# Third and fourth token block's output projections as one group of seven block products

## The chip, the cores and the metric

The kernel runs on one core of a Trainium2 chip. The metric is the time of one execution in microseconds of device time; for the kernel before, three runs took 2120.65, 2122.04 and 2125.73 us, median 2122.04. A profiled execution gives times of single instructions in the same unit.

## The reference

One decoder layer over 2048 tokens of width 1024, float32. What is computed, cut to its core:

```
h   = x * (1 + scale) + shift                    # modulation from c
q, k, v, r, a = split(h @ w_in)                  # 4 heads, dk 128, dv 256
o   = gated linear attention(q, k, v, a)         # chunks of 64, state over chunks
o   = rmsnorm(o) * norm_g * silu(r)              # the gated value
y   = o @ w_o                                    # the output projection, 1024 x 1024
x1  = layer_norm(alpha * x + (1 + gate) * y)
u,g = split(modulated(x1) @ w_up)                # 2 x 2816
x2  = (silu(causal_conv3(u)) * g) @ w_down
out = layer_norm(alpha * x1 + (1 + gate2) * x2)
```

## The kernel before

Tokens stand in four blocks (`tb` 0 to 3) of 512. Every large product is done with three matmuls of a rounded and a rest part (`mm3`, L109 to L112: high x high, high x low, low x high); `split` (L103) makes the two parts of a tile, a cast on ScalarE (ACT, L104) and a subtraction on VectorE (DVE, L107). A *unit* is a piece of weights of 128x2x512 that stands in SBUF with both parts; it serves 24 matmuls of 128x512. `unit` (L156) hands out the next, and `issue` (L131) loads those ahead of it, two ahead of the one in use, into four buffers. A unit of the list `stream` can be loaded raw into half of its buffer and split there in place (`inplace`), can be stored after the split (`keep_in`), or can be loaded whole with both parts (`kept`).

Many products are made as two-by-two blocks with seven block products instead of eight: rows and columns of tokens, inner dimension and output columns are halved, sums of blocks are formed of both operands first, and the results are added into the outputs while they are accumulated in PSUM. The up and down projections and the q, k, v, r projections of other blocks are done so, and in the stage of this change the output projection of token blocks 0 and 1 (`o_pair`, L1481, operands from `o_x`, L1465, which takes the sums of gated values in SBUF). Its seven products stand in the order `OP` = 1, 0, 5, 6, 3, 4, 2 (L1194); the weights' sums come from `wfc_d`, the plain ones from `wf_d`, both folded with the gate.

The stage of this change stands between the input projections and the up projection and has 38 units: 8 for q and k of token block 1 (`q_segment`, L1443), 14 for `o_pair`, and 8 each for `o_segment` (L1509) of token blocks 2 and 3, which multiply plainly: eight k-tiles of gated values from DRAM (`g_d`, loaded by `get`, L1211) by `wf_d`, loaded again for each block and split again. Between the matmuls of the units stand the 16 heads of the attention (four blocks by four heads): each is a row of steps (`head_l` loads, `head_s` scales, `head_t` transposes, `head_a` masks, `head_b` states, `head_c` products, `head_n` norm, `head_d` transposes and gates; L1224 to L1384). The results of the projection are evicted by VectorE into rows of x (`load_z`, L1433), normalised (`ln1`, `normalise`, L1386 on), stored to `zn_d`, transposed on TensorE and stored to `xm2_d` (`ln1_kt`, L1410) as operand of the up projection. For block 3 the rows come back from `zn_d` during the up projection (`ln1_out`, L1425, table `todo`, L1752).

TensorE's order is written by hand: `at_unit` (L392) puts a step at a position counted in units, and `quarter` (L409) runs steps that are due after each quarter of a unit. `B0` is the stage's first unit; `H_AT`, `STEP`, `STEPB` (L1579 on) place the heads, `XO_AT` the operands of the first pair, `GET` those of the plain projections, `LZ_AT`, `LN_AT`, `LT_AT` rows, norm and transposes, `F_AT` (L1615) what prepares the up projection (`first_w`, `part_end` with `x_first(0)`, `x_first(1)`, `first_w1`, `first_w2`). For the other engines and the DMA issues, all of which are on SyncE's queue (SP), the framework's planner chooses an order with priorities: program order, drawn forward by `high_priority(offset)`. Issues on one queue run in order, and one that waits holds up those behind it. The up projection is a loop of 44 rounds (`n`); in its products, and in those of the q, k and r projections before the stage (`r_iter`), `keep` (L445) copies PSUM banks out by ACT (L448).

```
H_AT = (0.25, 1.5, 2.75, 4, 5, 6, 7.25, 8.25, 9.75, 13.5, 14.0, 15.5, 17.5, 19.5, 21.5, 23.5)
SEG = (("Q", 1), ("OO", 0), ("O", 2), ("O", 3))
```

## Time and profile before

| what | value |
|---|---|
| median of three runs | 2122.04 us |
| the profiled execution's own time | 2121.6 us |
| its span, first to last instruction | 2119.9 us |
| granted TensorE clock, mean | 0.996 |
| TensorE busy | 2085.8 us, 98% |
| VectorE busy | 1529.5 us, 72% |
| ACT busy | 1003.4 us, 47% |
| GpSimd busy | 107.0 us, 5% |
| DMA | 546.24 MB, mean 258 GB/s |

In the groups of the profile a line has source line, engine, operation, output and input tiles, shape and count, then busy time, mean ns of one, and idle time of the engine before them with what ended it. A line of waits has who waited for whom, microseconds in total, how often, and the longest. Matmuls overlap, so a matmul's own duration is longer than the step from one to the next. L12 is line 12 of the kernel before.

### The profile page before, as it was taken

To read this page: it belongs to the slowest core of one execution; us is meant where nothing else is said; L and a number is where in the kernel's file an instruction comes from. 1 tells how busy PE (TensorE), PEld (TensorE's weight loads), DVE (VectorE), ACT (ScalarE), POOL (GpSimd) and SP (SyncE) were. 2 spreads that over 40 slices of the span, in tenths; PEclk is the share of its full clock that TensorE was granted. 3 is DMA by queue.
4 is the path that set the end of the run, shared out by engine and by line. 5 is a ranking of instruction groups with operands and counts; after the bars stand their busy time and mean duration, and the time that the engine had idled before them with its cause. 6 is when DMAs were issued, how large, how long until landed. Compare 5 with 4: busy or idle time off the path is not lost.

```text
span 2119.9 us, 26188 instructions
## 1 busy us (share of the span) xinstructions
PE 2085.8 (98%) x9381; PEld 1721.9 (81%) x9381; DVE 1529.5 (72%) x2022; ACT 1003.4 (47%) x1405; POOL 107.0 (5%) x254
## 2 busy tenths in 40 slices
PE   9999999999999998999999999999999999999998
PEld 7887887778888787888888888888888888888886
DVE  6855757776687667878777787666676796577557
ACT  4648636674555544644444454333333443344332
POOL 0000000001112201100000000000000000020001
PEclk9999999999999999999999999999999999999999
DMA  9787888788745885777756679877777897677562
GB/s 336 304 295 261 283 306 286 268 306 317 277 145 196 310 289 192 274 249 285 273 194 219 219 253 321 288 258 273 246 276 256 295 325 250 206 247 251 189 200 89
DMA packets 192035, 546.24 MB, mean 258 GB/s; under 512 B 24928, under 2 KB 33504, under 8 KB 186272
## 3 DMA queue, kind: packets, MB, share of 16 engines
q1 hardware_dynamic: 191904, 544.56, 73.5%
q8 instruction: 74, 1.21, 0.2%
q14 instruction: 57, 0.47, 0.1%
HBM read 357.58 MB, written 186.91 MB: 257 GB/s over the span
## 4 chain that ended last, share of the span: by engine, by line
PE 71%; DVE 3%; ACT 2%; DMA 2%; issue 1%; POOL 1%; SPq 0%; DVEq 0%; POOLq 0%; ACTq 0%
PE ps_mm L110 15%; PE ps_mm L112 15%; PE ps_mm L111 15%; PE ps_w L111 7%; PE ps_w L110 7%; PE ps_w L112 7%; PE ps_w L1326 1%; PE ps_w L1354 1%; PE ps_w L1356 1%; PE ps_w L1310 1%; DMA hl<-wf_d 1%; DMA A<-a_d 0%; PE ps_w L1375 0%; PE ps_w L1416 0%; ACT on L1369 0%
## 5 line engine op out<-in xcount | busy, mean ns | idle before, releaser
L110 PE MATMUL ps_mm<-xc,hl 128*128 128x512 f32 x920 | 361.8, 393 | 6.2 <-ACT u L448 4.5
L111 PE MATMUL ps_mm<-xc,hl 128*128 128x512 f32 x920 | 359.5, 391 | 0.0
L112 PE MATMUL ps_mm<-xc,hl 128*128 128x512 f32 x920 | 358.8, 391 | 0.0
L110 PEld LDWEIGHTS ps_mm<-xc,hl 128*128 128x128 f32 x920 | 173.5, 189 | 46.4 <-ACT u L448 6.6
L112 PEld LDWEIGHTS ps_mm<-xc,hl 128*128 128x128 f32 x920 | 173.4, 189 | 36.5 <-DVE hl L107 0.2
L111 PEld LDWEIGHTS ps_mm<-xc,hl 128*128 128x128 f32 x920 | 173.6, 189 | 36.1 <-issue 0.5
L110 PE MATMUL ps_w<-xc,hl 128*128 128x512 f32 x464 | 180.6, 389 | 0.0
L111 PE MATMUL ps_w<-xc,hl 128*128 128x512 f32 x464 | 180.5, 389 | 0.0
L112 PE MATMUL ps_w<-xc,hl 128*128 128x512 f32 x464 | 180.5, 389 | 0.0
L1655 DVE SCALAR_TENSOR_TENSOR ct<-U,cw_sb,ct 128x512 f32<-128x512 f32 x176 | 131.8, 749 | 22.8 <-ACT ct L1649 20.2
L104 ACT CAST hl<-wu 128x1024 fp32r<-128x1024 f32 x90 | 94.8, 1053 | 104.1 <-PE ps_mm L112 76.9
L448 ACT COPY u<-ps_mm 128x512 f32<-128x512 f32 x112 | 65.3, 583 | 159.4 <-PE ps_mm L112 152.0
L104 ACT CAST dhl<-raw 128x1024 fp32r<-128x1024 f32 x57 | 60.1, 1054 | 159.2 <-PE ps_mm L112 98.5
L107 DVE TENSOR_TENSOR hl<-wu,hl 128x1024 fp32r<-128x1024 f32 x90 | 110.0, 1222 | 30.2 <-ACT hl L104 29.9
L107 DVE TENSOR_TENSOR dhl<-raw,dhl 128x1024 fp32r<-128x1024 f32 x57 | 69.7, 1223 | 65.4 <-ACT dhl L104 65.4
L107 DVE TENSOR_TENSOR hl<-raw,hl 128x1024 fp32r<-128x1024 f32 (+1 forms) x63 | 69.3, 1104 | 56.1 <-ACT hl L104 55.8
L110 PE MATMUL ps_mm<-hl,xg 128*128 128x512 f32 x240 | 104.0, 433 | 3.6 <-DVE z L1526 3.6
L104 ACT CAST hl<-raw 128x1024 fp32r<-128x1024 f32 (+1 forms) x63 | 60.0, 955 | 99.4 <-PE ps_mm L112 42.1
L104 ACT CAST hl<-wg 128x1024 fp32r<-128x1024 f32 x56 | 59.0, 1053 | 97.6 <-PE ps_mm L112 85.0
L110 PE MATMUL ps_mm<-dhl 128*128 128x512 f32 x264 | 102.7, 389 | 0.0
L111 PE MATMUL ps_mm<-dhl 128*128 128x512 f32 x264 | 102.7, 389 | 0.0
L112 PE MATMUL ps_mm<-dhl 128*128 128x512 f32 x264 | 102.7, 389 | 0.0
(284 smaller groups left out, 4743.7 us busy)
## 6 DMA issues: line engine op xcount, KB each, us to landing
hc_d<-ct SPq DMA_DIRECT2D x154, 256.0 KB, 2.9
raw<-hc_d SPq DMA_DIRECT2D x70, 512.0 KB, 4.2
draw<-wc_d SPq DMA_DIRECT2D x70, 512.0 KB, 4.6
wu<-in_wup_dram SPq DMA_DIRECT2D x44, 512.0 KB, 5.3
wg<-in_wup_dram SPq DMA_DIRECT2D x44, 512.0 KB, 4.3
wh_d<-hl SPq DMA_DIRECT2D x22, 1024.0 KB, 4.8
hl<-wh_d SPq DMA_DIRECT2D x22, 1024.0 KB, 6.6
mraw<-in_mws_dram SPq DMA_DIRECT2D x40, 512.0 KB, 6.0
```

What stands on the lines that cost most here:

```text
L104: accs["copy"] = nc.scalar.copy(h, src)
L107: return nc.vector.tensor_tensor(l, src if lsrc is None else lsrc, h.bitcast(F32), op=ALU.subtract)
L110: nc.tensor.matmul(po, a[0], b[0], start=first, stop=False, skip_group_check=resumed)
L111: nc.tensor.matmul(po, a[0], b[1], start=False, stop=False, skip_group_check=resumed)
L112: return nc.tensor.matmul(po, a[1], b[0], start=False, stop=last, skip_group_check=resumed)
L448: return t, nc.scalar.copy(t, po)
L1310: nc.tensor.matmul(pav[:, i], KI[:, s * P:s * P + P], Q[:, s], start=True, stop=True)
L1326: nc.tensor.matmul(pst[:, s % 2 * DV:s % 2 * DV + DV], KTt[:, s * P:s * P + P], v[s], start=True, stop=True)
L1354: nc.tensor.matmul(pos_, at[:, i], v[s], start=True, stop=st is None)
L1356: nc.tensor.matmul(pos_, Q[:, s, 0:128], st, start=False, stop=True)
L1655: nc.vector.scalar_tensor_tensor(ct, U[:, o + i:o + i + 512], cw_sb[:, j, i:i + 1], ct, op0=ALU.mult, op1=ALU.add)
```

## The change

The plain projections of token blocks 2 and 3 are replaced by a second call of `o_pair`, with 14 units; `o_segment` is gone. The operands `XY` are made as follows. Products 1 and 0 take the gated values of block 2 as they are (`y_x`). `y_sums` forms the sums of the gated values in SBUF, makes the operand of product 5 from one of them, and stores the other four (`xo_d`) to DRAM; `y_load` loads these into half of the operand's own tile when a tile is free, and `y_put` splits them in place. The gated values are no longer stored (`g_d` is gone), so they stay in SBUF until `y_sums`, in buffers shared with those of earlier blocks (`head_r`).

The weight parts of the first `o_pair`, once split, are stored to `wq_d` (1 MB each, 14 of them), and the second `o_pair` loads them with both parts and splits nothing.

The transposes of block 2 no longer stand in the stage: `todo` now runs `ln1_out` for block 2 in rounds 3 to 6 of the up projection and for block 3 in rounds 7 to 10 (before 3 to 6), and `x_pre` in rounds 12 and 15 (before 9 and 12).

Positions are set anew throughout: heads 6 and 8 to 15 stand up to two units earlier, the stage's tables are new, and steps before the stage (`x_prep`, gates, modulation, weight folding) move by up to some six units. Several priorities are raised (`keep` from 0 to 600, others from 60, 150, 300 or 600 to 300, 600 or 1200), the order in which buffers of units take turns no longer shifts at turn 48, and two of the raw tiles of `x_first` stand in the heads' buffers in place of those of the rows.

The diff, cut:

```diff
@@ -220,7 +220,7 @@
...
     e_d = [[dram.tile([P, 1024], F32, name=f"e_d{t}_{h}") for h in range(NH)] for t in range(NTB)]
-    g_d = [[dram.tile([P, 1024], F32, name=f"g_d{t}_{h}") for h in range(NH)] for t in range(NTB)]
+    xo_d = {i: [dram.tile([P, 1024], F32, name=f"xo_d{i}_{r}") for r in range(2)] for i in (2, 3, 4, 6)}
     xm2_d = [[dram.tile([P, 2, TB], F32, name=f"xm2_d{t}_{k}") for k in range(4)] for t in range(NTB)]
@@ -444,7 +444,7 @@
...
-        with tc.high_priority(offset=0):
+        with tc.high_priority(offset=600):
@@ -1137,19 +1137,19 @@
...
-        R_AT = ((7.75, 10.25, 12.0), (42.75, 45.0, 45.75))
+        R_AT = ((9.75, 10.25, 12.25), (42.75, 45.0, 45.25))
...
-        WAW_AT = (11, 46.25, 54.25)
+        WAW_AT = (12.25, 45.75, 53.75)
...
-        GR_AT = (17, 48, 54.75)
+        GR_AT = (17, 48, 54.25)
...
-        XP_AT = (18.5, 22.5)
+        XP_AT = (16.5, 19.75)
@@ -1157,28 +1157,28 @@
...
-        M_AT = (36, 37.5, 38, 39, 40, 41, 41.75, 43.25, 51, 52, 53, 54, 55, 56, 57, 58)
-        MF_AT = (50.5, 49.5, 56.5, 62.0)
+        M_AT = (36, 36.5, 37.75, 37.75, 40, 41, 41.75, 43.25, 51, 52, 53, 54, 55, 56, 57, 58)
+        MF_AT = (50.0, 49.5, 57.5, 62.5)
...
-        at_unit(65, mod2)
+        at_unit(68.5, mod2)
...
-        G_AT = (54, 55.5, 56.5, 56.75, 58, 59.25, 60, 61.5, 62.25)
+        G_AT = (51.75, 55.5, 56.5, 57.25, 58.5, 59.25, 60, 61.75, 62.5)
...
-        WF_AT = ((69, 69.5, 70, 70.75), (75, 75.5, 76, 76.5))
-        WM_AT = ((73, 74), (77, 78))
+        WF_AT = ((69, 69.0, 70.0, 70.75), (72, 74.25, 75.5, 76.75))
+        WM_AT = ((72.0, 74.0), (82.75, 83.75))
...
-        E_AT = (84, 85.45, 86.7, 87.7)
+        E_AT = (83.25, 85.45, 87.7, 88.45)
@@ -1193,12 +1193,14 @@
...
         wraw = {0: 0, 1: 2, 3: 6}
-        for i in OP:
-            for u in range(2):
-                stream.append((wf_d[wraw[i] + u] if i in wraw else wfc_d[i][u], None, None, True))
-        for tb in (2, 3):
-            for n in range(8):
-                stream.append((wf_d[n], None, None, True))
+        KEEP = (1, 1, 1, 1, 1, 1, 1, 1, 1, 1, 1, 1, 1, 1)
+        for q in range(2):
+            for n, (i, u) in enumerate((i, u) for i in OP for u in range(2)):
+                src = wf_d[wraw[i] + u] if i in wraw else wfc_d[i][u]
+                if q == 0:
+                    stream.append((src, wq_d[n] if KEEP[n] else None, None, True))
+                else:
+                    stream.append((None, None, wq_d[n], False) if KEEP[n] else (src, None, None, True))
         at_unit(B0 - 6, lambda: (load_unit(), load_unit()))
@@ -1210,12 +1212,11 @@
...
             kind, tb = key
-            assert kind == "Q" or ("g", tb, pr) in made
             t = xg_tile()
...
                 r = raw_tile("xraw")
-                load(r, xm1_d[tb][pr] if kind == "Q" else g_d[tb][pr])
+                load(r, xm1_d[tb][pr])
             split(t[:, 0], t[:, 1], r)
@@ -1284,12 +1285,11 @@
...
         def head_r(H):
-            if H["tb"] == 1:
+            tag = (("sra", "sra", "srb", "srb"), (None,) * 4, ("sr2", "sr2", "srb", "srb"), ("sra", "sra", None, None))[H["tb"]][H["h"]]
+            if tag is None:
                 sr = raw_tile("sr").rearrange("p (s c) -> p s c", s=2)
-            elif H["tb"] == 0:
-                sr = ab.tile([P, 2, 512], F32, tag="sr", name="sr", bufs=4)
             else:
-                sr = ab.tile([P, 2, 512], F32, tag="sr2", name="sr", bufs=2)
+                sr = ab.tile([P, 2, 512], F32, tag=tag, name="sr", bufs=2)
             H["sr"] = sr
@@ -1373,15 +1373,11 @@
...
                 nc.tensor.transpose(pt[:, s * P:s * P + P], on[:, s, e * P:e * P + P], ident)
-            with tc.high_priority(offset=300):
+            with tc.high_priority(offset=600):
                 nc.vector.scalar_tensor_tensor(sr[:, e], pt, ng_sb[:, e:e + 1], sr[:, e], op0=ALU.mult, op1=ALU.mult)
...
                 return
-            made.add(("g", H["tb"], H["h"]))
-            if H["tb"] < 2:
-                gated[H["tb"], H["h"]] = sr.rearrange("p s c -> p (s c)")
-            else:
-                store(g_d[H["tb"]][H["h"]].rearrange("p (s c) -> p s c", s=2), sr)
+            gated[H["tb"], H["h"]] = sr.rearrange("p s c -> p (s c)")
 
@@ -1478,9 +1474,41 @@
...
 
-        def o_pair():
+        XY = [None] * 7
+        yraw = {}
+
+        def y_x(i):
+            for pr in range(2):
+                x_put(XY, i, pr, gated[2, pr + 2 * i], xg_tile())
+
+        def y_sums(pr):
+            b11, b21, b12, b22 = [gated[b, pr + h] for b in (2, 3) for h in (0, 2)]
+            store(xo_d[2][pr], b22)
+            add(nc.vector, b11, b12, b11, SUB)
+            r = z_tile("xo")
+            add(nc.vector, r, b22, b11, SUB)
+            x_put(XY, 5, pr, r, xg_tile())
+            store(xo_d[4][pr], b11)
+            add(nc.vector, b12, b22, b12, SUB)
+            store(xo_d[6][pr], b12)
+            add(nc.vector, b21, b21, r, SUB)
+            store(xo_d[3][pr], b21)
+            made.add(("y", pr))
+
+        def y_load(i):
+            assert ("y", 0) in made and ("y", 1) in made
+            yraw[i] = [xg_tile() for _ in range(2)]
+            for pr, t in enumerate(yraw[i]):
+                load(t[:, 1].bitcast(F32), xo_d[i][pr])
+
+        def y_put(i):
+            for pr, t in enumerate(yraw[i]):
+                x_put(XY, i, pr, t[:, 1].bitcast(F32), t)
+
+        def o_pair(q):
             into = {1: (0, 0), 0: (0, 0), 5: (1, 0), 6: (1, 1), 3: (0, 1), 4: (1, 1), 2: (1, 0)}
             seen = set()
+            X = (XO, XY)[q]
             for i in OP:
@@ -1493,11 +1521,11 @@
...
                         for k in range(2):
-                            xh, xl = XO[i][2 * u + k]
+                            xh, xl = X[i][2 * u + k]
                             mm3(banks[t], (xh[:, tk], xl[:, tk]), (wv[:, 0, k], wv[:, 1, k]),
...
                         if u == 1:
-                            z = zs_of[tb][t][:, cs_]
+                            z = zs_of[2 * q + tb][t][:, cs_]
                             with tc.high_priority(offset=0):
@@ -1560,7 +1566,7 @@
...
-                    src[i] = actp.tile([P, D], F32, tag="zs", name="xs", bufs=5)
+                    src[i] = actp.tile([P, 2, 512], F32, tag=("E", "qk")[i - 4], name="xs").rearrange("p s c -> p (s c)")
@@ -1576,9 +1582,9 @@
...
-        H_AT = (0.25, 1.5, 2.75, 4, 5, 6, 7.25, 8.25, 9.75, 13.5, 14.0, 15.5, 17.5, 19.5, 21.5, 23.5)
-        STEP = (-0.4, 0, 0.5, 0.6, 0.75, 0.2, 0.5, 0.85, 1, 0.5, 1.5, 1.6, 1.6, 2.3, 2.5)
-        STEPB = (-0.5, 0, 0.5, 0.75, 1, 0.25, 0.75, 1, 1.25, 0.75, 1.75, 2, 2, 2.75, 3)
+        H_AT = (0.25, 1.5, 2.75, 4, 5, 6, 7, 8.25, 9.5, 12.75, 13.5, 14.75, 16.75, 18.5, 20, 21.5)
+        STEP = (-0.4, 0, 0.5, 0.6, 0.75, 0.2, 0.5, 0.85, 1, 1.5, 1.5, 1.6, 1.6, 2.3, 2.5)
+        STEPB = (-0.5, 0, 0.5, 0.75, 1, 0.0, 0.25, 0.75, 1.0, 0.5, 1.75, 2, 2, 2.75, 3)
@@ -1589,38 +1595,37 @@
...
-        SEG = (("Q", 1), ("OO", 0), ("O", 2), ("O", 3))
-        XO_AT = (7, 8.75, 11, 12.75, 14.75, 16.5, 18.5)
+        SEG = (("Q", 1), ("OO", 0), ("OO", 1))
+        XO_AT = (7, 8.75, 10.75, 12.75, 14.75, 15.5, 18.0)
...
-        GET = ((20.5, 20.5, 22.25, 22.25), (28.5, 29.5, 30.0, 31.0))
-        for n, key in enumerate(SEG[2:]):
-            for pr in range(4):
-                u = GET[n][pr]
-                if key[0] == "O":
-                    u = max(u, H_AT[4 * key[1] + pr] + STEPB[-1] + 0.05)
-                at_unit(B0 + u, get, key, pr)
-        LZ_AT = ((5.75, 5.75, 5.75, 5.75), (10, 10, 11, 11), (21.5, 21.5, 21.5, 21.5), (27.5, 27.5, 27.5, 27.5))
-        BY_ACT = ((0, 1, 0, 1, 0, 1, 0, 1), (0, 1, 0, 1, 0, 1, 0, 0), (0, 1, 0, 1, 0, 1, 0, 1))
-        LN_AT = ((17, 17.25, 17.5, 18.25), (21, 21.25, 21.5, 21.75), (29, 29.25, 29.5, 29.75))
-        LT_AT = ((18.5, 18.75, 19, 19.25, 19.5, 19.75, 20, 20.25), (22.0, 22.25, 22.5, 23.25, 23.5, 23.75, 24, 24.25), (30, 30.25, 30.5, 30.75, 31, 31.25, 31.5, 31.75))
+        YX_AT = (19.75, 21.75)
+        YS_AT = (23.0, 23.0)
+        for n in range(2):
+            at_unit(B0 + YX_AT[n], y_x, 1 - n)
+            at_unit(B0 + max(YS_AT[n], H_AT[14 + n] + STEPB[-1] + 0.05), y_sums, n)
+        YL_AT = ((25.5, 26.75), (27.25, 28.5), (29.0, 30.25), (31.0, 32.25))
+        for n, i in enumerate((6, 3, 4, 2)):
+            at_unit(B0 + YL_AT[n][0], y_load, i)
+            at_unit(B0 + YL_AT[n][1], y_put, i)
+        LZ_AT = ((5.75, 5.75, 5.75, 5.75), (10, 10, 10.75, 11), (21.5, 21.5, 21.5, 21.5), (25.75, 25.75, 25.75, 25.75))
+        BY_ACT = ((1, 1, 0, 0, 1, 0, 1, 1), (0, 1, 1, 0, 0, 0, 0, 0), (0, 0, 0, 1, 0, 1, 1, 1))
+        LN_AT = ((17, 18.25, 17.5, 18.0), (21, 21.25, 21.5, 21.75), (32.5, 32.75, 33, 33.25))
+        LT_AT = ((18.5, 18.75, 19, 19.0, 20.5, 20.75, 20, 20.25), (22.0, 22.25, 22.5, 23.25, 23.5, 23.75, 24, 24.25), (40.25, 40.25, 40.25, 38, 40, 40, 40, 40))
...
-            for kt in range(KT):
+            for kt in range(KT if tb < 2 else 0):
...
-        F_AT = (31, 32, 34, 35, 36)
+        F_AT = (28, 29.5, 34, 32, 34.5)
...
-                if kind == "OO":
-                    o_pair()
-                else:
-                    (q_segment if kind == "Q" else o_segment)(tb)
+                (o_pair if kind == "OO" else q_segment)(tb)
@@ -1749,8 +1754,8 @@
...
-        todo = {3 + pr: [(ln1_out, NTB - 1, None, (pr,), True)] for pr in range(4)}
-        todo |= {9: [(x_pre, 1, 0)], 12: [(x_pre, 1, 1)]}
+        todo = {3 + pr + 4 * b: [(ln1_out, 2 + b, None, (pr,), True)] for b in range(2) for pr in range(4)}
+        todo |= {12: [(x_pre, 1, 0)], 15: [(x_pre, 1, 1)]}
...
```

35 lines of the change are left out of this document (7 added, 28 removed).

## The prediction

> **What bounds the kernel now.** First I read the page: the busy row of the engines and the chain of waits. In the busy row the numbers are microseconds, share of the span and instructions.
>
> ```profile
> span 2119.9 us, 26188 instructions
> PE 2085.8 (98%) x9381; PEld 1721.9 (81%) x9381; DVE 1529.5 (72%) x2022; ACT 1003.4 (47%) x1405; POOL 107.0 (5%) x254
> PE 71%; DVE 3%; ACT 2%; DMA 2%; issue 1%; POOL 1%; SPq 0%; DVEq 0%; POOLq 0%; ACTq 0%
> ```
>
> TensorE is busy almost throughout, so a matmul that goes away is worth its issue step, as long as nothing else becomes late. The busy time of one matmul (389 ns) is not that step, because matmuls overlap. The timeline of TensorE has both: 36 block matmuls in a row, first and last row here, start 489.07 and 497.00 us.
>
> ```profile
> 489.07 0.39 PE L110 MATMUL ps_mm<-xg,hl 128*128 128x512 f32 x1
> ...
> 497.00 0.39 PE L112 MATMUL ps_mm<-xg,hl 128*128 128x512 f32 x1
> ```
>
> That is 7.93 us for 35 steps, so 0.2266 us a matmul and 5.44 us for a unit of 24 matmuls. I number the units of the stage from 0 (481.2 us: the first k-major unit of the second block's q and k): before there are 38, of which 22 to 37 are the projections of the third and fourth block.
>
> Next the windows of this stage (units 0 to 7, 8 to 21, 22 to 37; columns: length, then busy time of PE, PEld, DVE, ACT and POOL, granted clock, DMA share, GB/s), and what TensorE waited for, first in the time before 481 us, then in the stage.
>
> ```profile
> 481.20:573.70 92.50, 89.76 (x442) 76.47 (x441) 58.47 (x102) 44.74 (x97) 12.39 (x35) 1.00 0.83 298
> 573.70:722.84 149.14, 145.48 (x727) 122.89 (x726) 122.16 (x205) 78.38 (x160) 25.90 (x53) 1.00 0.60 209
> 722.84:849.60 126.76, 118.05 (x557) 96.50 (x556) 86.27 (x117) 60.34 (x89) 15.15 (x33) 0.99 0.71 254
> ```
>
> ```profile
> PE ps_mm L110 <- ACT u L448: 5.6, 6, 2.2
> PE ps_mm L110 <- ACT p L448: 1.6, 2, 1.1
> ...
> PE ps_w L1375 <- ACT on L1369: 4.7, 3, 1.8
> PE ps_mm L110 <- DVE z L1526: 3.6, 1, 3.6
> PE ps_w L1416 <- ACT zs L1397: 2.5, 3, 1.0
> PE ps_w L1299 <- DVE sr L1377: 2.0, 1, 2.0
> ```
>
> ```profile
> 850.00:1240.00 390.00, 390.00 (x1738) 323.26 (x1738) 308.65 (x417) 179.69 (x244) 13.34 (x52) 1.00 0.69 243
> 783.88:849.60 65.72, 60.35 (x273) 49.09 (x272) 47.80 (x55) 29.20 (x29) 5.31 (x12) 0.97 0.61 223
> ```
>
> Behind the stage, in the up projection (first row), TensorE waits for nothing; the last ten units of the stage are the second row. So all that can still be gained lies in matmuls, in 7.2 us of waits for ACT's copies (`keep`) and some 13 us of waits in the stage.
>
> One thing comes on top of a wait: the matmuls after it step by 0.43 us for a while.
>
> ```profile
> 169.17 0.50 PE L110 MATMUL ps_mm<-xc,hl 128*128 128x512 f32 x1 [2.18 <-ACT u L448]
> ...
> 170.26 0.63 PE L110 MATMUL ps_mm<-xc,hl 128*128 128x512 f32 x1
> 170.69 0.63 PE L111 MATMUL ps_mm<-xc,hl 128*128 128x512 f32 x1
> 169.00:172.00 3.00, 2.83 (x8) 2.23 (x9) 3.00 (x4) 2.76 (x6) 0.00 (x0) 0.60 0.64 231
> 831.90:834.90 3.00, 3.00 (x9) 2.33 (x8) 3.00 (x4) 0.00 (x0) 0.00 (x0) 0.50 0.00 0
> ```
>
> The granted clock is 0.60 and 0.50 there. Some seven matmuls lose 0.2 us each, 1.4 us a time; it follows two of the `keep` waits and the 3.6 us wait. The Trainium skill (TensorE: Matmul & The Clock Gate, What's actually happening) has the clock fall after an idle window of about 3.4 us; here a wait of 2.18 us was enough, so the row decides, and by the page alone the two `keep` waits would have been 2.8 us cheaper.
>
> **The change part by part.** (1) *Matmuls.* The two eight-unit projections become one group of seven products of two units: 16 units become 14. 48 matmuls x 0.2266 = **-10.9 us**. The first pair's projection already has this form in units 8 to 21.
>
> (2) *Transposes moved.* The third block's 32 transposes go from the stage into the up projection, where the fourth block's are already. The chain of waits gives a group's step there:
>
> ```profile
> 920.70 0.87 PE ps_w L1416 x8
> zc<-zn_d SPq DMA_DIRECT2D x16, 128.0 KB, 3.7
> 526.94 1.30 PE ps_w L1310 x8
> 529.62 1.73 PE ps_w L1326 x8
> 532.74 0.87 PE ps_w L1375 x8
> ```
>
> 32 x 0.87/8 = 3.5 us leaves and returns: 0. With them move 16 loads and 8 stores on SP (the fourth block's 16 loads land in 3.7 us each) and 8 evictions, now all on ACT, which is busy under half of that time; nothing waits for them before the second half of the up projection. What does go is the wait of such transposes for ACT's normalised rows at 800 us: two of the three waits of L1416 above, the longest of 1.0 among them, so 1.0 + 0.8 of 2.5 us: **-2 us**. If that cover is missing in the up projection, each lateness counts in full, since TensorE has no slack there; I keep 0 to +3.
>
> (3) *VectorE and ACT.* A 128x512 eviction costs 0.68 us, a split 1.05 us on ACT and 1.22 us on VectorE, a sum of two gated tiles 1.22 us:
>
> ```profile
> L107 DVE TENSOR_TENSOR hl<-hl 128x1024 fp32r<-128x1024 f32 x14 | 17.1, 1219 | 9.7 <-ACT hl L104 9.6
> L1389 DVE BATCH_NORM_STATS2 bst<-zs 128x6 f32<-128x512 f32 x13 | 8.3, 669 | 0.0
> L1526 DVE SCALAR_TENSOR_TENSOR zs<-zs,ps_mm 128x512 f32<-128x512 f32 x8 | 5.4, 682 | 0.0
> L352 DVE TENSOR_TENSOR xs<-xs 128x1024 f32<-128x1024 f32 x4 | 4.9, 1222 | 0.0
> L352 DVE TENSOR_TENSOR wu<-wu 128x512 f32<-128x512 f32 x1 | 0.7, 693 | 0.0
> ```
>
> Evictions 28 for 16 (+8.2 us), eight sums (+9.8), operand splits 14 for 8 (+7.3), weight splits 14 for 30 (-19.5), four block evictions less (-3): +3 us for VectorE over the stage, and ACT loses ten casts. What counts is where it falls. After the last head (position 24.5 of 36) there are 11.5 units, 62.6 us. VectorE then has 24 evictions (16.3), half to all of the sums and their splits (6 to 12), eight operand splits (9.8), statistics of the third block (8 x 0.67 + 0.8 = 6.2), the 16 sums and splits that build the up projection's operands (19.6), and its first weights (2.4 + 4 x 0.7 = 5.2): 63 to 69 us. It is full. Consecutive ones overlap by some 7%, so 59 to 65; with imperfect filling I take 5 us of TensorE wait, 0 to 15. It stands in the place of the 3.6 us wait for `z` and its 1.4 us of slow clock, which arise now at just this spot and for this reason: **0**.
>
> (4) *DMA.* In units 8 to 21 every weight part, once split, is stored (14 x 1 MB), and in units 22 to 35 it is loaded whole, 1 MB in place of 0.5 MB. The stores and loads of the gated values stay equal (16 of 0.5 MB). For 22 to 35 I add up: 12 weight loads (two are issued ahead) 12.6 MB, stores and loads of sums 4.2 + 4.2, rows of x 4.2, normalised rows 4.2, transposed rows 2.1, two gates 1.0, operands and weights of the up projection 6.3: 38.8 MB. TensorE needs for these units 14 x 5.44 = 76.2, plus what is left of heads 14 and 15 (a head is 1.30 + 0.87 by the rows under (2), 1.73 each for its states, its masked scores and its states' products, and 0.44 for four transposes, 7.8 in all; left are one head and 2.6) and 32 transposes (3.5) and switches between types (some 2): 92 us. So 38.8/92 = 420 GB/s is asked for. The nearest rows are the fullest 10 us and the busiest 50 us:
>
> ```profile
> 530.00:540.00 10.00, 10.00 (x53) 8.58 (x52) 6.36 (x12) 4.71 (x12) 0.58 (x4) 1.00 1.00 396
> 700.00:750.00 50.00, 46.92 (x241) 38.94 (x240) 36.15 (x63) 25.19 (x46) 9.29 (x22) 1.00 0.87 301
> 835.00:900.00 65.00, 65.00 (x288) 53.80 (x287) 57.99 (x79) 37.29 (x46) 6.51 (x17) 1.00 0.62 222
> ```
>
> The third block's normalised rows and one weight store (3.1 MB) may slip into the up projection, which has room (222 GB/s). 35.7 MB is 90 us at 396 GB/s and 119 us at 301: a lateness of 0 to 27 us. I take **+3 us**, near the upper rate, because the weights have a prefetch of two units (10.9 us against a landing of 6.6 us for 1 MB) and the queue mostly waited for buffers, not for transfers:
>
> ```profile
> SPq L141 <- PE ps_mm L112: 77.2, 19, 10.3
> hl<-wh_d SPq DMA_DIRECT2D x22, 1024.0 KB, 6.6
> wh_d<-hl SPq DMA_DIRECT2D x22, 1024.0 KB, 4.8
> ```
>
> The Trainium skill (DMA: Bandwidth & Descriptors, Where 436 GB/s comes from) has HBM bind at about 358 GB/s a core. The row of 396 GB/s is above that; by the page 35.7 MB would be 100 us, and the term +8 instead of +3.
> The 14 new stores stand in SP's one queue and wait for VectorE's half of the split; behind them stand the next weight load and the heads' loads. Units 8 to 21 have 209 GB/s and a DMA share of 0.60, so 14.7 MB more fits, and I take 0 there (-0 to +5).
>
> (5) *The way over DRAM.* Four of the seven operands go out and come back. From the last head's gate (24.5) to the product that needs the first of them (28) there are 19 us. The way takes 0.75 (gate) + 3 x 1.22 (sums) + 2.3 (split of the fifth operand) + 3.8 (store) + 5.5 (load) + 2.3 (split) = 18 us, durations from the rows here and below. Just hidden: **+1**, 0 to 5.
>
> ```profile
> g_d<-sr SPq DMA_DIRECT2D x8, 512.0 KB, 3.8
> xraw<-g_d SPq DMA_DIRECT2D x8, 512.0 KB, 5.5
> L1377 DVE SCALAR_TENSOR_TENSOR sr<-ps_w,ng_sb,sr 128x512 f32<-128x512 f32 x7 | 5.1, 747 | 4.2 <-PE ps_w L1375 4.2
> ```
>
> (6) *Priorities and positions.* `keep` is drawn forward on ACT (offset 0 to 600) and the steps before 481 us are set at other units. Bounds: all 7.2 us and 2.8 us of slow clock go (-10), or as much again is made elsewhere by the moved steps (+5). I take **-4**, the larger waits gone and some new small ones. The heads stand closer (16 by 24.5 instead of 26.5); their waits for ACT (4.7 us) I leave, -5 to +5.
>
> Sum: -10.9 - 2 + 0 + 3 + 1 - 4 = **-12.9 us**. The profiled execution took 2121.6 us (span 2119.9), 0.4 us under the median shown (2122.0). 2121.6 - 12.9 = 2108.7; I say 2109.
>
> **The rivals.** *More goes than the matmuls* (the copy waits and the head waits vanish, DMA costs nothing): -10.9 - 2 - 10 - 3 = -26 to -20, some 2098. For it: the first pair shows units without any wait on operands. Against: the last 11 units are full on VectorE.
> *VectorE becomes the bound of the last units.* Each split also waits 0.7 us on average for ACT's half (9.7 us over 14 in the row above). 14 such idle times on a full engine are 10 us more than I took: 2109 + 10 = 2119, no change that can be measured. For it: the 3.6 us wait arose there with less work (47.80 us busy in the last 65.72).
> *DMA becomes the bound of units 22 to 35* (the other side). If the queue moves no more than the 301 GB/s of the busiest 50 us, 35.7 MB takes 119 us against 92, +27 where I took +3: 2109 + 24 = 2133, slower. It decides from a landing of the 1 MB weight loads above 10.9 us, twice a unit; the loss passes the gain at about 320 GB/s. Against: the 301 GB/s came with a share of 0.87, not 1.00.
> *The change doesn't do what it says*: fewer matmuls are certain from the loops, so only their place could be wrong; I give that nothing of its own.
>
> **How the numbers follow.** A measurement of this kernel tells about 0.3%, 6.4 us, from no change: the borders are 2115.7 and 2128.4. My forecast (2102 to 2115) has 0.56, more gone 0.17, VectorE's bound 0.18, DMA's 0.09. Faster is the first two, 0.73; same 0.18; slower 0.09. The range runs from 2096 (most of "more gone") to 2123 (VectorE's bound with its upper spread) and leaves out some 0.15. The forecast's own range is 2102 to 2115.
>
> **What would show it.** Right: 9333 matmul records (48 fewer), 14 units from 22 to 35 in about 95 us, DMA in them at 350 to 400 GB/s, waits for L448 under 4 us before the stage, none in the up projection. Wrong: waits of block matmuls for weight loads (DMA, the new parts) of over a microsecond a unit, or for VectorE's operands at the products 6 and 3; weight loads that land after more than 10.9 us; or an up projection that begins with waits for its own operands.

## The result, and the profile after

The changed kernel took 2109.39 us (median of five runs, 2108.16 to 2115.09) against 2122.04 us (five runs, 2120.65 to 2126.9) for the kernel before on the same chip: ratio 0.9939, interval 0.992 to 0.9958, 12.65 us less. Predicted were 2109.0 us and faster. The total is right, by 0.4 us; several of its terms are not, and their errors nearly cancel, so that closeness is luck.

The busy row and the chain of waits of the page after:

```profile
span 2107.0 us, 26146 instructions
PE 2074.5 (98%) x9333; PEld 1713.0 (81%) x9333; DVE 1532.0 (73%) x2028; ACT 997.2 (47%) x1401; POOL 109.8 (5%) x254
PE 82%; DVE 6%; DMA 5%; ACT 4%; issue 2%; POOL 0%; SPq 0%; DVEq 0%; ACTq 0%; POOLq 0%
```

48 matmuls are gone, as counted in advance. TensorE is still busy for 98% of the span, and VectorE as long as it was (1529.5 us before, 1532.0 now, the 3 us more that the prediction counted). So what is left to find lies in places where TensorE waits.

The stage after in windows (units 0 to 7, 8 to 21, 22 to 35, then the last 11.5 units alone and 40 us inside them; columns as in the prediction):

```profile
484.49:573.73 89.24, 89.24 (x441) 76.56 (x440) 57.00 (x101) 43.61 (x97) 12.01 (x35) 1.00 0.92 332
573.73:729.92 156.19, 153.26 (x761) 129.79 (x759) 131.13 (x223) 83.90 (x175) 31.01 (x63) 0.99 0.81 296
729.92:826.99 97.07, 93.88 (x444) 77.49 (x443) 70.81 (x97) 37.37 (x57) 12.39 (x22) 1.00 0.90 335
764.30:826.99 62.69, 59.50 (x261) 48.20 (x260) 47.56 (x62) 20.84 (x20) 5.75 (x12) 1.00 0.86 332
760.00:800.00 40.00, 36.81 (x167) 29.48 (x166) 27.81 (x34) 9.07 (x11) 0.76 (x1) 1.00 0.99 377
```

Units 22 to 35 take 97 us (about 95 predicted) at 335 GB/s (350 to 400 predicted): 32.5 MB, where 35.7 were counted. Units 8 to 21 became 7 us longer than before, since more of the heads stand in them now, and carry the weight stores (209 GB/s before, 296 now) without harm. The waits of TensorE after: before the stage (first two rows), in the stage, and in the first 63 us of the up projection (last two rows):

```profile
PE ps_mm L110 <- ACT u L448: 9.4, 7, 3.2
PE ps_mm L110 <- ACT p L448: 0.5, 2, 0.3
...
PE ps_w L1375 <- ACT on L1369: 2.3, 3, 1.0
PE ps_mm L112 <- DVE xg L107: 1.5, 1, 1.5
PE ps_mm L110 <- DVE z L1533: 0.9, 1, 0.9
PE ps_mm L110 <- DVE zs L352: 0.8, 1, 0.8
PE ps_w L1299 <- DVE sr L1377: 0.3, 1, 0.3
...
PE ps_w L112 <- DVE hl L107: 2.0, 1, 2.0
PE ps_mm L110 <- ACT xc L104: 0.7, 1, 0.7
```

Three things are to be seen. The copy waits (L448) before the stage didn't shrink. TensorE's idle time in the stage (length less busy time, summed over the three windows) fell from 15.1 to 6.1 us. And the up projection, which began without any wait before, now waits for its own operands.

To compare kernels stretch by stretch I use one measure. The *nominal* time of a stretch is its matmuls, each by the usual step of its shape (0.2266 us for 128x512); the *excess* is the rest of the time from start to start: waits, slow clock after them, and switches between types. It comes from one profile of each kernel.

| kernel | median us | ratio to before, interval | excess before stage | units 0–7 | units 8–21 | from 22 on | first 60 us of up projection |
|---|---|---|---|---|---|---|---|
| before | 2122.04 | | 17.9 | 3.9 | 7.4 | 14.0 | 0.0 |
| after | 2109.39 | 0.9939, 0.992–0.9958 | 21.2 | 0.6 | 8.0 | 4.9 | 5.9 |
| e_plain | 2113.65 | 0.9964, 0.9948–0.998 | 21.6 | 0.9 | 6.6 | 3.7 | 0.0 |
| e_plainH | 2122.49 | 1.0005, 0.9994–1.0016 | 22.3 | 1.0 | 12.5 | 11.7 | 0.0 |
| e_plainP | 2115.91 | 0.9975, 0.996–0.999 | 16.4 | 0.6 | 11.3 | 3.5 | 0.0 |
| b_tr | 2121.77 | 0.9998, 0.9989–1.0007 | 16.1 | 3.0 | 8.7 | 13.3 | 0.0 |
| e_prekeep0 | 2110.88 | 0.9943, 0.9926–0.9961 | 22.7 | 1.4 | 6.8 | 4.9 | 7.2 |
| e_nokeep | 2113.86 | 0.9961, 0.9947–0.9976 | 18.9 | 0.9 | 9.4 | 9.6 | 5.9 |
| e_dma | 2120.64 | 0.9989, 0.9978–1.0 | 27.0 | 1.4 | 6.4 | 14.1 | 5.4 |
| e_xf | 2112.06 | 0.9948, 0.9935–0.9961 | 14.9 | 0.9 | 5.9 | 12.0 | 4.3 |
| e_ln | 2108.59 | 0.9936, 0.9919–0.9954 | 20.0 | 0.9 | 10.9 | 5.3 | 6.4 |
| e_nostat | 2110.12 | 0.9941, 0.9927–0.9954 | 23.5 | 0.6 | 6.0 | 6.8 | 6.4 |
| e_act | 2113.94 | 0.9961, 0.9947–0.9974 | 23.0 | 0.7 | 9.0 | 10.3 | 7.6 |
| e_actln | 2111.14 | 0.9951, 0.9936–0.9965 | 20.1 | 0.9 | 9.8 | 11.0 | 5.0 |

The kernel before ran again beside each group of experiments, with medians from 2121.4 to 2122.1 us; the ratios are to those. The column before the stage scatters from 14.9 to 27.0 us among the kernels that have the changed program there (all but before, b_tr and e_prekeep0). So a difference of a few microseconds in that column of single profiles tells nothing. A profiled execution need not lie at the median either: that of e_plainP took 2110.2 us, 5.7 us under it, that of e_xf 5.4 us under, those of e_act and e_plainH 4.7 and 3.3 us over theirs. Gains are therefore taken from the medians, and the columns only say where in the kernel the time lies.

### The profile page after: what moved, and what is told of

The parts are those of the page before. It is cut to its first block, busy times and chain, and to the rows that moved or that the text cites. A ratio compares the mean times of both kernels' runs of the same rounds, so it can differ in the third digit from the quotient of the medians.

```text
span 2107.0 us, 26146 instructions
## 1 busy us (share of the span) xinstructions
PE 2074.5 (98%) x9333; PEld 1713.0 (81%) x9333; DVE 1532.0 (73%) x2028; ACT 997.2 (47%) x1401; POOL 109.8 (5%) x254
## 4 chain that ended last, share of the span: by engine, by line
PE 82%; DVE 6%; DMA 5%; ACT 4%; issue 2%; POOL 0%; SPq 0%; DVEq 0%; ACTq 0%; POOLq 0%
PE ps_mm L110 17%; PE ps_mm L112 17%; PE ps_mm L111 17%; PE ps_w L112 8%; PE ps_w L111 8%; PE ps_w L110 8%; PE ps_w L1354 1%; PE ps_w L1326 1%; PE ps_w L1356 1%; PE ps_w L1310 1%; DMA A<-a_d 1%; DMA mraw<-in_mws_dram 1%; PE ps_w L1412 1%; DVE hl L107 1%; PE ps_w L1375 1%
## 5 line engine op out<-in xcount | busy, mean ns | idle before, releaser
L110 PEld LDWEIGHTS ps_mm<-xc,hl 128*128 128x128 f32 x920 | 173.5, 189 | 50.6 <-ACT u L448 10.9
L448 ACT COPY u<-ps_mm 128x512 f32<-128x512 f32 x112 | 65.3, 583 | 161.9 <-PE ps_mm L112 153.4
L112 PEld LDWEIGHTS ps_w<-xc,hl 128*128 128x128 f32 x464 | 87.1, 188 | 20.5 <-DVE hl L107 2.4
```

The costliest lines, as they stand in the source:

```text
L110: nc.tensor.matmul(po, a[0], b[0], start=first, stop=False, skip_group_check=resumed)
L112: return nc.tensor.matmul(po, a[1], b[0], start=False, stop=last, skip_group_check=resumed)
L448: return t, nc.scalar.copy(t, po)
```

## Experiments: which edit brings the time

**The seven products taken back (e_plain).** Everything of the change stays (positions, priorities, gated values in SBUF, transposes of the third block in the up projection), but the second pair is multiplied in sixteen plain units with operand positions of their own, no weights are kept, the buffers of units take turns as in the kernel before, and what prepares the up projection stands about two units later.

```diff
-        SEG = (("Q", 1), ("OO", 0), ("OO", 1))
+        SEG = (("Q", 1), ("OO", 0), ("O", 2), ("O", 3))
-        for q in range(2):
+        for q in range(1):
...
+        for tb in (2, 3):
+            for n in range(8):
+                stream.append((wf_d[n], None, None, True))
...
-        F_AT = (28, 29.5, 34, 32, 34.5)
+        F_AT = (31.25, 32, 34, 35, 36)
```

> The changed kernel with its second pair made plainly again: 16 units with eight products in place of 14 with seven, gated values still taken from SBUF, weights loaded and split (none kept), the positions of the heads and of all earlier steps as in the changed kernel; steps at the end of the stage two units later. Theory (a matmul that goes away is worth its step): 48 matmuls x 0.2266 = 10.9 us more than the changed kernel's 2109.4, less up to 4 us of waits that go with the fuller last units: 2116 to 2120. Rival (the positions made the gain, the seven products only moved the bound to VectorE and DMA): within 3 us of the changed kernel, 2107 to 2112.

Measured: 2113.65 us, 4.3 us above the changed kernel and 8.4 below the one before, between the two expectations. By the profile, e_plain has 10.9 us more nominal time in the stage than after, but 2.3 us less excess there and 5.9 us less at the start of the up projection. So the seven products save what was counted, and 8.2 us of it return as excess in the two profiles, 6.6 us by the medians (10.9 - 4.3). Of the 2.3 us some 1.5 are one stretch of slow clock (634.1 to 637.5 us in after), which another execution can lack; the 5.9 us are what stays. The other 8.4 us of the gain come without the seven products.

**The heads' positions taken back as well (e_plainH).** On top of e_plain, the positions of the heads, of the first pair's operands and of the norms and transposes of block 0 are those of before, and so is the choice of the engine that evicts the transposes of blocks 0 and 1 (`BY_ACT`).

```diff
-        H_AT = (0.25, 1.5, 2.75, 4, 5, 6, 7, 8.25, 9.5, 12.75, 13.5, 14.75, 16.75, 18.5, 20, 21.5)
+        H_AT = (0.25, 1.5, 2.75, 4, 5, 6, 7.25, 8.25, 9.75, 13.5, 14.0, 15.5, 17.5, 19.5, 21.5, 23.5)
...
-        XO_AT = (7, 8.75, 10.75, 12.75, 14.75, 15.5, 18.0)
+        XO_AT = (7, 8.75, 11, 12.75, 14.75, 16.5, 18.5)
```

> The second pair in sixteen plain units with the priorities of the changed kernel, but with the positions of the heads' steps, of the first pair's loads and of the first norms as in the kernel before. Theory (the new positions of the heads are what took the stage's excess from 25 to 11 us): the excess over the stage goes back to 19 to 25 us, and the time to 2117 to 2122 us. Rival (the priorities, or the other buffers of the gated halves, did it): the excess stays at 10 to 15 us, the time at 2112 to 2116 us.

Measured: 2122.49 us, as long as the kernel before. The stage's excess goes from 11.2 to 25.1 us, where before has 25.3. The waits in the stage, first of e_plain, then of e_plainH, show it:

```profile
PE ps_w L1375 <- ACT on L1369: 2.3, 3, 1.0
PE ps_mm L110 <- DVE z L1558: 1.8, 1, 1.8
```

```profile
PE ps_w L1375 <- ACT on L1369: 6.8, 4, 3.1
PE ps_mm L110 <- DVE z L1558: 1.8, 1, 1.8
...
```

The largest is the heads' wait for ACT's normalised output (`on`), which was 4.7 us before. The rest of the excess is slow clock behind such waits (three stretches in this profile's stage, one of them of double length, and none in that of e_plain) and steps without a listed wait; 5.9 us of the 13.9 come in units 8 to 21 and 8.0 from unit 22 on, where more heads stand when they are spread as before. The intervals of e_plain and e_plainH don't touch: what was set back (heads, first operands, first norms and transposes with their engine; they weren't separated) is worth about 9 us.

**The priorities taken back (e_plainP).** e_plain with the priorities of seven places in the stage as before (two of them here).

```diff
@@ head_l, head_t, head_a, state, head_c, head_d, copies in q_segment @@
-            with tc.high_priority(offset=1200):
+            with tc.high_priority(offset=60):
...
-            with tc.high_priority(offset=600):
+            with tc.high_priority(offset=150):
```

> The second pair in sixteen plain units with the new positions, but with the priorities of the seven places in the stage (head's first rows, transposes, mask, state, gate, the evictions of the weights' last part) as in the kernel before. Theory (positions alone did it): the excess over the stage stays at 10 to 15 us, and the time at 2112 to 2116 us. Rival (the priorities did it): the excess goes back to 19 to 25 us, and the time to 2117 to 2122 us.

Measured: 2115.91 us, 2.3 us over e_plain with intervals that overlap widely; the stage's excess is 15.4 us. The positions carry most of the gain; a share of the priorities of 2 or 3 us stays open.

**The transposes alone (b_tr).** The kernel before, with only the third block's transposes moved to the up projection.

```diff
-            for kt in range(KT):
+            for kt in range(KT if tb < 2 else 0):
...
-        todo = {3 + pr: [(ln1_out, NTB - 1, None, (pr,), True)] for pr in range(4)}
-        todo |= {9: [(x_pre, 1, 0)], 12: [(x_pre, 1, 1)]}
+        todo = {3 + pr + 4 * b: [(ln1_out, 2 + b, None, (pr,), True)] for b in range(2) for pr in range(4)}
+        todo |= {12: [(x_pre, 1, 0)], 15: [(x_pre, 1, 1)]}
```

> The kernel before with one part of the change alone: the third block's 32 transposes run in rounds 3 to 6 of the up projection, the fourth's in rounds 7 to 10, and the preparation of the second half in rounds 12 and 15. Theory (the transposes' own 3.5 us leave and return, and only the waits of these transposes go): 1 to 3 us faster than the kernel before, 2119 to 2121. Rival (they make room for VectorE and ACT ahead of the full end of the stage, so that the 5 us of wait and slow clock there go as well): 2114 to 2117.

Measured: 2121.77 us, no difference (the interval reaches from 2.3 us faster to 1.5 us slower). The waits in its stage:

```profile
PE ps_mm L110 <- DVE z L1526: 5.4, 1, 5.4
PE ps_w L1375 <- ACT on L1369: 4.6, 3, 1.8
```

The waits of L1416 for normalised rows are gone, as said, but the wait for `z` is 5.4 us in place of 3.6: VectorE's lateness at the end of the stage is met elsewhere.

**The time before the stage (e_prekeep0).** The changed kernel with the positions before the stage and the priority of `keep` as before.

```diff
-        with tc.high_priority(offset=600):
+        with tc.high_priority(offset=0):
...
-        R_AT = ((9.75, 10.25, 12.25), (42.75, 45.0, 45.25))
+        R_AT = ((7.75, 10.25, 12.0), (42.75, 45.0, 45.75))
```

> The changed kernel with all steps ahead of the stage at the positions of before and the bank copies (keep) at priority offset 0 again. Theory (these two parts of the change cost 3.3 us, since the stage begins at 484.5 us and not at 481.2): the stage begins at about 481.2 again, 2106. Rival (the copies' priority helps inside the up projection or at its start, or the positions help the stage): 2109 to 2113.

Measured: 2110.88 us, not to be told from 2109.39. The stage begins at 486.1 us, not at 481.2 as the theory had it. These edits neither bring nor cost anything that six runs show.

## Experiments: what the limits are worth

**No kept weights (e_nokeep).** Weights of the second pair are loaded raw and split again.

```diff
-        KEEP = (1, 1, 1, 1, 1, 1, 1, 1, 1, 1, 1, 1, 1, 1)
+        KEEP = (0,) * 14
```

> The changed kernel without keeping the weight parts: nothing is stored in units 8 to 21, and the second pair loads 0.5 MB raw for each unit and splits it. Theory (VectorE is the full engine of the last units): 14 more splits, 17 us of VectorE and 15 us of ACT in a stretch of 97 us with VectorE busy for 70.8: 3 to 10 us slower than the changed kernel, 2112 to 2119. Rival (DMA, with a share of 0.90 in these units, sets their pace): 22 MB less to move, 2 to 5 us faster, 2104 to 2107.

Measured: 2113.86 us, 4.5 us longer; the intervals still overlap at their ends, but the profile agrees. Units 22 to 35 in this kernel:

```profile
729.31:831.07 101.76, 94.50 (x444) 77.06 (x442) 86.65 (x111) 50.27 (x70) 13.45 (x22) 1.00 0.75 271
```

VectorE is busy for 86.65 of 101.76 us, against 70.81 of 97.07 with kept weights, and ACT for 50.27 against 37.37. The load on DMA falls from 335 to 271 GB/s, and no gain from that is to be seen. So keeping the weights in DRAM seems to pay because it relieves VectorE and ACT; which of the two counts, this run doesn't separate.

**More DMA (e_dma).** The changed kernel with 14 more transfers of 0.5 MB, DRAM to DRAM, one written into each of the units 22 to 35; nothing reads them, and so nothing ties them to those units.

```diff
+                    if q == 1:
+                        junk(u + 2 * OP.index(i))
...
+        def junk(n):
+            load(junk_d[n], wf_d[n % 8])
```

> The changed kernel with an additional transfer of 0.5 MB from DRAM to DRAM in each of the units 22 to 35, 7.3 MB in all, whose data nobody reads. Theory (DMA is used to 0.90 in these units, but the two units of prefetch hide that; the spare is about 0.10 x 97 us x 380 GB/s = 3.7 MB): the rest, 3.6 MB, is 10 us of queue, of which some arrives at TensorE as waits for weights and operands: 2112 to 2122. Rival (DMA is far from deciding): 2108 to 2111.

Measured: 2120.64 us, 11.3 us longer. But the transfers didn't go where they were meant to go. All 14, with first and last start, and those issued from 735 to 841 us:

```profile
L1542 SPq DMA_DIRECT2D junk_d<-wf_d x14: 473/538/975, 397.4 to 827.9; - x14
junk_d<-wf_d SPq DMA_DIRECT2D x4, 512.0 KB, 10.8
```

The planner issued ten of them before unit 22 (three at 397 to 413 us, seven at 606 to 685 us) and four at 812 to 828 us. The window of units 22 to 35, and from the timelines the largest new wait and the casts of the last product's operands:

```profile
734.91:841.10 106.19, 97.26 (x444) 78.99 (x443) 72.20 (x98) 36.52 (x56) 14.03 (x22) 0.97 0.95 357
825.54 0.47 PE L110 MATMUL ps_mm<-hl,xg 128*128 128x512 f32 x1 [3.56 <-ACT hl L104]
822.16 1.98 ACT L104 CAST xg<-xg 128x1024 fp32r<-128x1024 f32 x2
```

9.2 of the 11.3 us lie in these units (excess 14.1 instead of 4.9): units 33 and 34 take 9.2 and 10.2 us instead of 5.4. The casts of the last product's operands on ACT (third row) start at 822.16 us, in after at 809.57. The operands' loads land after 8.3 us (median, 785 to 830 us) instead of 5.0, and in this kernel the planner also has the scaling of the last rows and casts for the up projection ahead of these casts. The wait's row names the cast behind them, of a weight, which ends at 825.09 us; an eviction on VectorE ends at 825.44, so which of the two let the matmul go stays open. So neither theory nor rival was put to the test: the 11 us are the price of this order of the queues, with four more transfers in units 32 to 34, and how much room DMA has in units 22 to 35 isn't shown.

## Experiments: the start of the up projection

The first half of the up projection's operands (`x_first(0)`, called from `part_end`) is made at unit 29.5, the second (`x_first(1)`) at 32. Loads of the second half stand on SP's queue behind the stores of the normalised rows, and its eight operations on VectorE behind the last evictions. VectorE after, at the boundary (826.99 us), where each row is one or two operations and brackets hold idle time:

```profile
825.83 0.69 DVE L352 TENSOR_TENSOR z<-z,ps_mm 128x512 f32<-128x512 f32 x1 [0.67 <-PE ps_mm L112]
827.26 1.23 DVE L107 TENSOR_TENSOR hl<-wu,hl 128x1024 fp32r<-128x1024 f32 x1 [0.74 <-ACT hl L104]
828.40 1.22 DVE L352 TENSOR_TENSOR xs<-xs 128x1024 f32<-128x1024 f32 x1
829.54 0.68 DVE L352 TENSOR_TENSOR z<-z,ps_mm 128x512 f32<-128x512 f32 x1
830.14 1.22 DVE L352 TENSOR_TENSOR xs<-xs,xc 128x1024 f32<-128x1024 f32 x1
831.27 1.22 DVE L107 TENSOR_TENSOR hl<-wg,hl 128x1024 fp32r<-128x1024 f32 x1
```

The second half's work begins at 828.40 us, after the up projection itself. The longest wait there, the 2.0 us for `hl`, ends with the split in the last row: a weight part of the up projection, which stands behind two of the second half's sums. Five runs look for what holds it.

**Both halves earlier (e_xf).**

```diff
-        F_AT = (28, 29.5, 34, 32, 34.5)
+        F_AT = (26.75, 27.0, 34, 32, 34.5)
```

> The changed kernel with the first half of the up projection's operands made from position 27.0 (its first weights from 26.75) in place of 29.5 and 28. Theory (VectorE is idle for some 9 us between 784 and 803 us, while the loads of this half stand on the DMA queue behind loads that wait for operand buffers, and is then full from 803 to 850, which makes the waits at the start of the up projection): the loads leave some 15 us earlier, VectorE fills its idle time, the 5.9 us at the start of the up projection shrink to 2 or less: 2104 to 2107. Rival (DMA is full from 760 to 800 us, with a share of 0.99, and only passes the lateness on to weights or operands): 2108 to 2113, with waits of block matmuls inside the stage in their place.

Measured: 2112.06 us. The start of the up projection loses 4.3 us instead of 5.9, but in the stage there are new waits for the operands of the second pair:

```profile
PE ps_mm L112 <- DVE xg L107: 3.1, 1, 3.1
PE ps_mm L110 <- ACT xg L104: 2.5, 1, 2.5
```

The work of VectorE and ACT only changed places: units 29 and 30 take 8.3 and 11.0 us, in after 5.4 and 7.2.

**The norm of the last rows later (e_ln).** Its stores no longer stand ahead of the loads.

```diff
-        LN_AT = (..., (32.5, 32.75, 33, 33.25))
+        LN_AT = (..., (34.25, 34.5, 34.75, 35))
```

> The changed kernel with the third block's four norms at positions 34.25 to 35 in place of 32.5 to 33.25, behind the second half of the up projection's operand step at 34. Theory (the norms' stores wait for ACT on the one DMA queue, from 807 to 820 us, and hold up the four loads behind them, so that the up projection begins with 5.9 us of waits and slow steps): the loads leave earlier, 2 to 5 us faster, 2104 to 2107. Rival (VectorE is full from 803 us to 850 us whenever the loads come): no change, 2108 to 2111.

Measured: 2108.59 us, no difference that can be told. The loads leave at 815.7 and 816.1 us instead of 820.5 and 823.5, and VectorE begins the second half at 826.10 us, 3.3 us before the boundary (829.38 us) instead of 1.4 us behind it. TensorE's wait for VectorE's `hl` there falls from 2.0 to 0.5 us. Yet the excess at the start is 6.4 us: in its place stand waits for ACT, 1.7 us for casts of weights and 2.3 us for copies (L448). ACT now scales the last rows at that time; their stores leave at 824.4 to 831.6 us.

**The statistics left out (e_nostat).** Leaves out the mean and variance of the last rows, so its output differs there; 6.2 us of work go from VectorE.

```diff
-            for i in range(2):
+            for i in range(2 if stats else 0):
...
+                nc.gpsimd.memset(mv, 1.0)
```

> The changed kernel without VectorE's statistics of the third block's first norm: the eight bn_stats and four aggregations are left out and mean and variance set to one, so that this block's rows are normalised by constants; all else is as it was. It takes 6.2 us of VectorE's work out of the stretch in which it is full. Theory (VectorE's fullness makes the 5.9 us of waits at the start of the up projection): they shrink by 4 to 6 us, 2103 to 2106. Rival (the lateness of the loads makes them): 2108 to 2111.

Measured: 2110.12 us, excess at the start 6.4 us, with 2.5 us of it one wait for a split of the second half. The last three loads, too, left earlier (815.5 to 818.0 us instead of 820.5 to 826.7). VectorE at that place:

```profile
828.04 0.69 DVE L352 TENSOR_TENSOR z<-z,ps_mm 128x512 f32<-128x512 f32 x1 [0.67 <-PE ps_mm L112]
829.40 0.69 DVE L352 TENSOR_TENSOR z<-z,ps_mm 128x512 f32<-128x512 f32 x1 [0.67 <-PE ps_mm L112]
830.48 1.22 DVE L107 TENSOR_TENSOR hl<-wg,hl 128x1024 fp32r<-128x1024 f32 x1 [0.40 <-ACT hl L104]
831.63 1.22 DVE L352 TENSOR_TENSOR xs<-xs 128x1024 f32<-128x1024 f32 x1
```

VectorE has idle time now (0.67 us before each eviction) and doesn't use it, because the planner's order has the second half behind the evictions, which wait for TensorE. A fuller or emptier engine is not the point here; its order is.

**The statistics on ACT (e_act), and with the later norm too (e_actln).** The last evictions give the row sums, ACT squares, GpSimd does the small steps; the output stays that of the reference.

```diff
+                                    nc.vector.scalar_tensor_tensor(z, a, f, b, op0=ALU.mult, op1=ALU.add,
+                                                                   accum_out=sums2[t][:, c:c + 1])
...
+                nc.scalar.activation(sq, z[:, i * 512:i * 512 + 512], AF.Square, bias=sm[:, 2:3], accum_out=sm[:, i:i + 1])
```

> The changed kernel with the statistics of block 3 off VectorE alone (the sums come with the last evictions, ScalarE squares), the scaling where it was. With the run that moves the scaling alone, it tells the two limits apart. Theory of two limits: the loads still leave at 820 to 827 us, the excess at the start of the up projection stays at 4 to 7 us and the time at 2108 to 2111 us. Rival (VectorE alone is the limit): the excess falls to 1 to 3 us, the time to 2104 to 2107 us.

> The changed kernel with both things that stand ahead of the last operands of the up projection's first product taken off together: the statistics of block 3 leave VectorE (its last eviction of each chunk gives the sums, ScalarE squares them), and the scaling of block 3 stands at positions 34.25 to 35, so that its stores are behind the loads of the second half of x_first. Theory (the 5.9 us at the start of the up projection have two limits, each of which alone hides the other: the loads at 821 to 827 us and VectorE at 824 to 838 us): the loads leave at about 815 us, the splits are done by 830 us, the excess there falls to 1 to 2 us and the time to 2103 to 2107 us. Rival (something third, the single buffers between the two halves of x_first or the planner's order, holds the second half): the excess stays at 5 to 7 us and the time at 2108 to 2112 us.

Measured: 2113.94 and 2111.14 us; neither theory's gain came. In e_actln the loads left at 817 us and the order had the second half between the last evictions, yet VectorE reached it at 832.4 us, 1.8 us before the boundary of this run (834.2 us). ACT, then VectorE, in e_actln:

```profile
823.51 1.24 ACT L1394 ACTIVATE zs<-zs,sm 128x1024 f32<-128x1024 f32 x1 [0.17 <-POOL sm L1393]
824.66 0.71 ACT L1389 ACTIVATE sq<-zs,sm 128x512 f32<-128x512 f32 x1
...
827.52 1.24 ACT L1394 ACTIVATE zs<-zs,sm 128x1024 f32<-128x1024 f32 x1 [2.06 <-POOL sm L1393]
828.67 1.03 ACT L104 CAST xc<-xc 128x1024 fp32r<-128x1024 f32 x1
829.60 1.04 ACT L104 CAST hl<-wu 128x1024 fp32r<-128x1024 f32 x1
```

```profile
830.68 1.22 DVE L107 TENSOR_TENSOR hl<-wu,hl 128x1024 fp32r<-128x1024 f32 x1 [4.15 <-ACT hl L104]
831.82 0.68 DVE L352 TENSOR_TENSOR z<-z,ps_mm 128x512 f32<-128x512 f32 x1
832.42 1.22 DVE L352 TENSOR_TENSOR xs<-xs 128x1024 f32<-128x1024 f32 x1
```

VectorE idles 4.15 us for ACT's cast of a weight part; the cast stands in ACT's queue behind the squares and the scaling, and these wait 2.06 us for GpSimd. In both runs most of what was lost lies ahead of the boundary (excess from unit 22 on 10.3 and 11.0 us instead of 4.9), with one wait of 2.9 us for a bank whose eviction stands on VectorE behind a split that waits for ACT. So the norm holds up the engine that has it, on ACT as on VectorE. What was shown is a negative: not the loads alone (e_ln), not the loads together with 6 us less work on VectorE (e_nostat), and not the norm on ACT. A norm that stands behind the second half on every queue wasn't tried, so whether the 5.9 us can be had stays open.

## Why the prediction was right, and where not

By the medians the products with all that hangs on them brought 4.3 us, where the terms (1), (3), (4) and (5) add up to 6.9; positions, priorities and transposes brought 8.4 us, where (2) and (6) add up to 6. The errors of +2.6 and -2.4 us cancel. That the sum met the measured time within 0.4 us is luck.

(1) *Matmuls*: right. The nominal time over the whole span fell by 10.9 us, as predicted, and no other shape lost or gained a matmul.

(2) *Transposes moved*, -2 us: 0 by b_tr, whose interval doesn't exclude -2; its waits speak against it. The cover in the up projection held. But the wait that was to go came back at `z` (3.6 to 5.4 us): I had taken a wait for independent that was one lateness of VectorE, met at whichever of its results came first.

(3) *VectorE at the end*, 5 us new in the place of 5 us before: the size is near, the place wrong. The list of 59 to 65 us for the last 62.6 us took both halves of the up projection's operands to be made in them. VectorE was busy for 47.56 us of them; the second half slid behind the boundary. The waits for `z` and `zs` are 1.7 us in the stage, and 5.9 us of excess stand at the start of the up projection, one of the signs named as making the prediction wrong. Not fullness but the order of the queues sets it: with 6 us of statistics gone the excess stayed (e_nostat).

(4) *DMA*, +3: 0 in after, since no block product of units 22 to 35 waits for a weight load. How near the bound on the other side is stays open, since e_dma put only four of its transfers there. After, 335 GB/s are asked for on the mean, under the 377 GB/s that the queues gave over 40 us at a share of 0.99. (The rate below which the loss passes the gain comes out of the prediction's own terms at some 330 GB/s, not 320.) The Trainium skill (DMA: Bandwidth & Descriptors, Where 436 GB/s comes from) has HBM bind at about 358 GB/s a core, though it also quotes 425 GB/s measured for one transfer of 16 MB; the row of 377 GB/s is above the first figure, so the measurement decides.

(5) *The way over DRAM*, +1: the size is right, the reason in part. It is the 1.5 us wait for `xg` at 794.6 us, in unit 30, the operand of product 3, and one of the signs named as wrong; that unit is 1.8 us longer than 5.44. The operand's cast on ACT waits for its load until 790.3 us and is done at 791.3; its split stands on VectorE behind two evictions and starts only at 793.4. So the order on VectorE has as much to do with it as the way over DRAM.

(6) *Priorities and positions*, -4 before the stage and 0 for the heads: both wrong, in opposite directions. The copy waits went from 7.2 to 9.9 us in the profile, and e_prekeep0 shows no effect of these edits (its few runs alone would not exclude 4 us). The heads' positions, which I left at 0 with -5 to +5, are, with the first operands, norms and transposes, worth about 9 us (e_plain against e_plainH); the stage's excess fell from 25.3 to 13.5 us with them. This is the step that failed: I looked at the 4.7 us of waits for `on` and not at the excess of the stage, which holds the slow clock after them and the crowding from unit 22 on.

The rivals: *VectorE becomes the bound* didn't come with kept weights; without them 4.5 us were lost (e_nokeep), with VectorE and ACT both fuller. *DMA becomes the bound* didn't come. *More goes than the matmuls* was half true: more did go in the stage, by the heads, and more than half of the matmuls' own gain was lost again, most of it at the start of the up projection.

## What to carry over

Saving matmuls in one stage saves their steps only if the engines that prepare the next stage have their work done before the boundary: here 10.9 us of TensorE's time brought 4.3. Where side work is spread between matmuls, its positions can be worth as much as the algebra; look at the time over the nominal steps, stretch by stretch, and not at the listed waits alone. When a piece of work holds up an in-order queue, moving it to another engine can move the hold-up with it, as here. And where a planner sets the order, an edit can land elsewhere than where it is written: most of the additional transfers of e_dma left 50 us or more ahead of their units.
